# Softmax weights turned by VectorE and transfers within SBUF instead of TensorE transposes

## The chip, the core and the metric

The kernel runs on one core of a Trainium2 chip. A core has TensorE (PE: matrix products into PSUM), VectorE (DVE), ScalarE (ACT), GpSimd (POOL) and SyncE (SP), each with a queue of its own that it works through in order, and 16 DMA engines that move data between memories. PE stands for the matrix products and PEld for the loads of stationary operands that go with them. The metric is the device time of one execution in microseconds (us), lower is better.

## What is computed

One encoder layer over 256 tokens of width 2048, in float32. The part that matters here is the attention group: twelve query heads of 128, four key and value heads (three queries share one), a window of 128 tokens to each side, a bias by distance, and a sink logit in the denominator.

```
q, k, v, u = split(rmsnorm(x) @ w_in)
s = (q @ k.T) * 128**-0.5 - slope * |t - s|        # -1e30 outside the window
m = max(max(s), sink)
p = exp(s - m);  p = p / (sum(p) + exp(sink - m))
out = p @ v                                        # per head: 256 x 256 weights, 256 x 128 values
x = x + concat(rmsnorm(out), rmsnorm(fourier(u))) @ w_out
x = x + conv_ffn(rmsnorm(x));  y = rmsnorm(x)
```

The scores come out with the queries on the partitions, so that the softmax runs along the free dimension. The product with the values sums over the keys, so it needs the weights with the keys on the partitions: each head's 256 x 256 weights have to be transposed once.

## The kernel before

Every float32 product is made of three products of rounded halves: a tensor is split into a high half (a copy to float32r on ScalarE) and a low half (the difference, on VectorE). The weights of the layer come in units of 1 MB: SP loads a unit (`load`, L172, issue in L177) into one of three raw buffers, `split` (L179) has ScalarE write the high half (L185) and VectorE the low one (L186), and TensorE multiplies. The order on every engine is written out by hand. For unit i, `unit(i, work)` (L423) issues what is listed `before` unit i, then unit i's matrix products, then what is listed `beside` it, then the split of unit i + 2 (and with it the load of unit i + 5, as soon as its raw buffer is read), then what is listed `behind` it. Each engine works in this order, so whatever stands in `beside` on VectorE or ScalarE is ahead of the split of unit i + 2.

Units 0 to 3 hold the Fourier input, 4 to 7 the values, 8 to 23 the keys and queries (one k, then three q, four times; `OPENING` and `QK_ORDER`, L45 to L50), 24 to 39 the output projection. A q or k unit is 32 products of 512 or 256 columns (L395, L397). The attention of a head whose q stands in unit s is spread over the units after it (L748 to L778):

- s + 1: the query is added up and split (`qk_out` L633, `qk_parts` L642; the addition is L637, the halves L234 and L235; for a key L637, L639, L652, L653)
- s + 2: the scores, six products (L663), `scores_out` (L671: bias and maximum, L679 to L684) on VectorE, and behind the split the exponentials on ScalarE (`exps`, L687)
- s + 3: `weigh` (L700): VectorE adds the sink, takes the reciprocal (L702, L703) and scales both halves of the weights (L706)
- s + 4: `turn` (L708): four TensorE transposes of 128 x 128 (L713) into one PSUM bank, listed before the unit's products; `turn_out` (L719): ScalarE copies the bank to the high half (L725), VectorE writes the low one (L726)
- s + 5: `values` (L729): six products (L735) ahead of the unit's own; `values_out` writes the head's output as halves (L492, L234, L235).

So every unit of this stage has work of several heads. Below, the heads of one group of three are called A, B and C in order. In `beside` the order before is: the query's `qk_out`, `turn_out`, `weigh`, the key's `qk_out` and `qk_parts`, `scores_out`, `values_out`. The Fourier group (L516 to L590) runs in units 5 to 13 and uses buffers of the tag `sc` as well. The tag `sc` has four buffers of 128 x 512, the halves of the turned weights two each.

Of the kernel before, what the change touches and what calls it, by code (L numbers as in the profile page):

```python
# [8 lines left out]
F32 = mybir.dt.float32  # L9
F32R = mybir.dt.float32r  # L10
AF = mybir.ActivationFunctionType
ALU = mybir.AluOpType

P = 128
D = 2048
S = 256
# [80 lines left out]
def block_kernel(  # L97
# [18 lines left out]
    nc = tc.nc  # L116
# [6 lines left out]
    dn = ctx.enter_context(tc.tile_pool(name="dn", bufs=4, space=bass.MemoryType.PSUM))  # L123

    def f32(ap):
        return ap.bitcast(F32)
# [13 lines left out]
    def bank(pool, name):  # L140
        return pool.tile([P, 512], F32, tag=pool.name, name=name)
# [63 lines left out]
    for n, size in enumerate(U_LOADS[1:], 1):  # L205
        k = sum(U_LOADS[:n])
# [15 lines left out]
    ident = base.tile([P, P], F32, tag="ident", name="ident")  # L222
    make_identity(nc, ident)

    ps = bank(dn, "ps_warm")
# [21 lines left out]
    for c in range(4):  # L247
        t = base.tile([P, 4, 512], F32R, tag=f"hT{c}", name=f"hT{c}")
# [45 lines left out]
    k = 0  # L294
# [15 lines left out]
    ph = pa.enter_context(tc.tile_pool(name="pa", bufs=1))  # L310
# [103 lines left out]
    before, beside, behind = {}, {}, {}  # L414

    def at(when, i, f, *a):
        when.setdefault(i, []).append((f, a))
# [136 lines left out]

    def fourier_rows_out():
        for g in range(NG):
            t = ph.tile([P, 512], F32, tag="sc", name=f"uf{g}", bufs=4)[:, 0:S]
            if g % 2:
                nc.scalar.activation(t, held.pop(("f", g))[:, 0:S], AF.Copy)
            else:  # L560
                nc.vector.tensor_copy(t, held.pop(("f", g))[:, 0:S])
            us.append(t)
# [39 lines left out]
    at(beside, 8, fourier_weights_out)  # L602
    at(before, 7, fourier_rows)
    at(beside, 7, fourier_rows_out)
    at(beside, 8, lambda: rows_out(v_hi, v_lo, ps_v))
    at(behind, 8, distances)

    def fourier_channels_steps():
        for g in range(NG):
            i = 9 + g  # L610
            at(beside, i, fourier_channels_copy, g)
            at(beside, i + 1, fourier_channels_join, g)
            at(behind, i + 1, fourier_channels_out, g)
        at(beside, 15, total_scale, "f", FW)
# [15 lines left out]
    qk_sb, st = {}, {}  # L630
    sq_a = ph.tile([P, S], F32, tag="sq", name="sq_a")

    def qk_out(kind, h, ps):  # L633
        tmp = ph.tile([P, S], F32, tag="tmp", name=f"tmp_{kind}{h}", bufs=2)
        nc.scalar.activation(tmp, ps[:, S : 2 * S], AF.Copy)
        add = ph.tile([P, S], F32, tag="add", name=f"add_{kind}{h}", bufs=2)
        nc.vector.tensor_tensor(add, ps[:, 0:S], tmp, ALU.add)  # L637
        if kind == "k":
            nc.vector.tensor_tensor(add, add, r1b, ALU.mult)  # L639
        st["add", kind, h] = add  # L640
# [30 lines left out]
    def scores_out(h):  # L671

        ps = st.pop(("s", h))
        sc = ph.tile([P, 512], F32, tag="sc", name=f"sc{h}", bufs=4)
        mx = ph.tile([P, 2], F32, tag="mx", name=f"mx{h}", bufs=2)
        neg = ph.tile([P, 2], F32, tag="neg", name=f"neg{h}", bufs=2)
        for b in range(2):
            s = slice(b * S, (b + 1) * S)
            nc.vector.tensor_tensor_reduce(  # L679
                sc[:, s], ps[:, s], rel[:, s], -float(SL[h]), -3e38, ALU.add,  # L680
                ALU.max, mx[:, b : b + 1],
            )
        nc.vector.tensor_tensor(neg, mx, rq_neg, ALU.mult)
        nc.vector.tensor_scalar(neg, neg, sink_neg[:, h : h + 1], None, ALU.min)  # L684
        st["sc", h] = sc, neg
# [20 lines left out]
            nc.vector.tensor_scalar(sc[:, s], sc[:, s], ex[:, b : b + 1], None, ALU.mult)  # L706

    def turn(h):  # L708
        ps = st["t", h] = bank(dn, f"ps_t{h}")
        sc = st.pop(("sc", h))[0]  # L710
        for sb in range(2):
            for b in range(2):
                nc.tensor.transpose(  # L713
                    ps[:, b * S + sb * P : b * S + (sb + 1) * P],
                    sc[:, b * S + sb * P : b * S + (sb + 1) * P],
                    ident,
                )

    def turn_out(h):  # L719
        ps = st.pop(("t", h))  # L720
        pt = [
            ph.tile([P, 512], F32R, tag=f"pt{q}", name=f"pt{q}{h}", bufs=2)
            for q in range(2)
        ]
        nc.scalar.activation(pt[0], ps, AF.Copy)  # L725
        nc.vector.tensor_tensor(pt[1], ps, f32(pt[0]), ALU.subtract)  # L726
        st["p", h] = pt

    def values(h, pool):  # L729
# [19 lines left out]
    for i in range(N_QK, N_OUT + 8):  # L749
        heads = {i - s: h for (kind, h), s in slot_of.items() if kind == "q"}  # L750
        new = [kh for kh, s in slot_of.items() if i - s == 1]
        if i - 9 in range(NG):
            at(before, i, fourier_channels, i - 9)
        if 5 in heads:
            at(before, i, values, heads[5], mm if i < N_OUT else dn)
        if 4 in heads:
            at(before, i, turn, heads[4])
        if i == 15:
            at(before, i, total, sq_f, "f")
        if 2 in heads:  # L760
            at(before, i, scores, heads[2])

        for kind, h in new:
            if kind == "q":
                at(beside, i, lambda k=kind, h=h: qk_out(k, h, st.pop(("ps", k, h))))
        if 4 in heads:
            at(beside, i, turn_out, heads[4])
        if 3 in heads:
            at(beside, i, weigh, heads[3])
        for kind, h in new:  # L770
            if kind == "k":
                at(beside, i, lambda k=kind, h=h: qk_out(k, h, st.pop(("ps", k, h))))
            at(beside, i, qk_parts, kind, h)
        if 2 in heads:
            at(beside, i, scores_out, heads[2])
            at(behind, i, exps, heads[2])
        if 5 in heads:
            at(beside, i, values_out, heads[5])  # L778

    fourier_channels_steps()  # L780
    for n, (kind, h) in enumerate(QK_ORDER):
# [57 lines left out]
    for n, (c, kq) in enumerate(OUT_ORDER):  # L839
        i = N_OUT + n  # L840
# [14 lines left out]
        if kq >= 2:  # L855
            part = "a" if kq == 2 else "f"
            ps = ps_a[c] if kq < 3 else ps_a[c, "f"]
# [307 lines left out]
    for q in range(2):  # L1165
        kind, j = items[q]
        ps = bank(mm, f"ps_{kind}{j}")
# [16 lines left out]
    for n, it in enumerate(items):  # L1184
# [8 lines left out]
        if it[0] in ("gate", "val"):  # L1193
            kind, j = it
            ps = bank(mm, f"ps_{kind}{j}")
# [4 lines left out]
        if it[0] == "product":  # L1200
            kind, g, c, p = it
            hi, lo = halves.pop(it)
            both = c == 2
            shape = (2, 1024) if both else (4, 512)
            for cc in (0, 1) if both else (c,):
# [5 lines left out]
                ps = bank(mm, f"ps_{p}{g}{cc}")  # L1211
# [6 lines left out]
        else:  # L1218
            kind, g, c = it
            hi, lo = halves.pop(up_index[n])  # L1220
            ps = [bank(mm, f"ps_l{g}{c}{b}") for b in range(2)]
# [10 lines left out]
    i = up_index[n]  # L1232
# [156 lines left out]
```

## Time and profile before

| | |
|---|---|
| time, median of 3 runs | 905.74 us (905.70 to 905.91) |
| the profiled execution's own time | 905.91 us |
| its span | 904.1 us |
| mean granted clock of TensorE | 0.998 |
| instructions | 12736 |
| DMA moved | 214.86 MB, mean 238 GB/s |
| SP's queue (q1) | 184.29 MB in 28592 packets |

The profile is one execution. Its page gives the busy time of every engine, and the chain of waits that ended last: followed back from the last instruction, at each step to what released it. The timeline lists instructions with start and duration; what stands in brackets is how long the engine was idle ahead of it, and what ended that. A name such as pt<-ps_t says what is written and what is read, L and a number the line of the kernel. SPq is SP's queue of DMA issues.

### The profile page before, as it was taken

Reading aid. Unit: us, or ns where it says so; the run is one execution under the profiler, and the core shown is the slowest. Engines: PE = TensorE matmul, PEld = TensorE weight load, DVE = VectorE, ACT = ScalarE, POOL = GpSimd, SP = SyncE. Lnnn points to the kernel's source line nnn. Section 1 sums busy time; section 2 is a strip of 40 time slices with the busy share of each in tenths; the row PEclk is TensorE's granted clock in tenths of the full one; section 3 lists DMA queues with packets and bytes.
Section 4 is the critical chain, followed back from the end, with each engine's and each line's share of the span. In section 5 each row is a group of like instructions: output and inputs, shape, how many; then the busy total and the mean of one; then the engine's idle time right before and its main releaser. Section 6 shows DMA issues by size and latency. Waiting matters only on the chain.

```text
span 904.1 us, 12736 instructions
## 1 busy us (share of the span) xinstructions
PE 895.6 (99%) x5064; PEld 808.5 (89%) x5064; DVE 746.0 (83%) x894; ACT 546.7 (60%) x661; POOL 51.6 (6%) x65
## 2 busy tenths in 40 slices
PE   9999999999999999999999999999999999999996
PEld 7899999888899999999999999999999999999885
DVE  7569888666668877889887998878988789998996
ACT  7757677555455656556565565566655566656544
POOL 0001111000000000000000000000000000000004
PEclk9999999999999999999999999999999999999999
DMA  9964544456568678677898779887888988779652
GB/s 359 343 232 142 187 155 171 145 182 227 192 242 272 231 242 252 187 256 235 271 265 271 245 258 285 261 278 238 274 250 244 312 263 263 242 240 289 213 198 94
DMA packets 32908, 214.86 MB, mean 238 GB/s; under 512 B 3632, under 2 KB 4016, under 8 KB 8528
## 3 DMA queue, kind: packets, MB, share of 16 engines
q1 hardware_dynamic: 28592, 184.29, 54.9%
q0 software_dynamic: 4112, 29.49, 17.5%
q8 instruction: 40, 0.66, 0.3%
q10 hardware_dynamic: 144, 0.26, 0.1%
q14 instruction: 20, 0.16, 0.0%
HBM read 211.93 MB, written 2.10 MB: 237 GB/s over the span
## 4 chain that ended last, share of the span: by engine, by line
PE 95%; DVE 2%; POOL 1%; issue 1%; ACT 0%; POOLq 0%; ACTq 0%; DVEq 0%
PE ps_val L395 17%; PE ps_gate L395 17%; PE ps_gate L397 8%; PE ps_val L397 8%; PE ps_q L395 5%; PE ps_P L1106 3%; PE ps_P L1108 3%; PE ps_P L1107 3%; PE ps_N L1106 2%; PE ps_N L1108 2%; PE ps_N L1107 2%; PE ps_u L289 2%; PE ps_q L397 2%; PE ps_a L378 2%; PE ps_a L380 2%; PE ps_a L379 2%
## 5 line engine op out<-in xcount | busy, mean ns | idle before, releaser
L186 DVE TENSOR_TENSOR parts<-raw,parts 128x2048 fp32r<-128x2048 f32 (+1 forms) x129 | 293.2, 2273 | 47.1 <-ACT parts L185 46.4
L185 ACT ACTIVATE parts<-raw 128x2048 fp32r<-128x2048 f32 (+1 forms) x129 | 245.6, 1903 | 44.5 <-PE ps_a L380 12.4
L395 PE MATMUL ps_val<-hU,parts 128*128 128x512 f32 x688 | 227.7, 382 | 0.0
L395 PE MATMUL ps_gate<-hU,parts 128*128 128x512 f32 x688 | 227.3, 382 | 0.0
L397 PE MATMUL ps_val<-hU,parts 128*128 128x256 f32 x688 | 187.5, 273 | 0.0
L397 PE MATMUL ps_gate<-hU,parts 128*128 128x256 f32 x688 | 186.9, 273 | 0.0
L395 PEld LDWEIGHTS ps_val<-hU,parts 128*128 128x128 f32 x688 | 130.0, 189 | 18.1
L395 PEld LDWEIGHTS ps_gate<-hU,parts 128*128 128x128 f32 x688 | 130.0, 189 | 18.1
L397 PEld LDWEIGHTS ps_val<-hU,parts 128*128 128x128 f32 x688 | 132.0, 192 | 0.8
L397 PEld LDWEIGHTS ps_gate<-hU,parts 128*128 128x128 f32 x688 | 131.8, 192 | 0.9
L884 ACT ACTIVATE ft_g<-ps_gate 128x256 f32<-128x256 f32 x43 | 16.5, 384 | 112.5 <-PE ps_gate L397 109.9
L395 PE MATMUL ps_q<-hT,parts 128*128 128x512 f32 x192 | 62.6, 384 | 0.0
L884 ACT ACTIVATE ft_v<-ps_val 128x256 f32<-128x256 f32 x43 | 16.5, 384 | 73.4 <-PE ps_val L397 73.4
L1106 PE MATMUL ps_P<-parts_P,op_P 128*128 128x512 f32 x144 | 54.7, 380 | 0.0
L1107 PE MATMUL ps_P<-parts_P,op_P 128*128 128x512 f32 x144 | 54.6, 379 | 0.0
L1108 PE MATMUL ps_P<-parts_P,op_P 128*128 128x512 f32 x144 | 54.6, 379 | 0.0
L397 PE MATMUL ps_q<-hT,parts 128*128 128x256 f32 x192 | 50.4, 273 | 0.0
L992 DVE TENSOR_TENSOR parts_N<-sumw,parts_N 128x2048 fp32r<-128x2048 f32 x18 | 41.2, 2288 | 9.9 <-ACT parts_N L991 9.9
L1106 PE MATMUL ps_N<-parts_N,op_N 128*128 128x512 f32 x108 | 41.0, 380 | 0.0
L1107 PE MATMUL ps_N<-parts_N,op_N 128*128 128x512 f32 x108 | 40.9, 379 | 0.0
L1108 PE MATMUL ps_N<-parts_N,op_N 128*128 128x512 f32 x108 | 40.9, 379 | 0.0
L395 PEld LDWEIGHTS ps_q<-hT,parts 128*128 128x128 f32 x192 | 36.1, 189 | 4.7
(344 smaller groups left out, 1555.0 us busy)
## 6 DMA issues: line engine op xcount, KB each, us to landing
raw<-in_w_up SPq DMA_DIRECT2D x86, 1024.0 KB, 6.2
raw<-in_w_in SPq DMA_DIRECT2D x20, 1024.0 KB, 4.9
sumw<-in_w_down POOLq DMA_DIRECT2D x18, 1024.0 KB, 8.4
raw<-in_w_out SPq DMA_DIRECT2D x16, 1024.0 KB, 4.8
raw<-in_w_down_late SPq DMA_DIRECT2D x4, 1024.0 KB, 5.3
u_raw<-in_u_in SPq DMA_DIRECT2D x4, 768.0 KB, 10.9
raw<-in_w_down_last SPq DMA_DIRECT2D x4, 768.0 KB, 4.2
u_raw<-in_u_in SPq DMA_DIRECT2D x7, 384.0 KB, 6.4
```

Of the source, the lines that this page charges most:

```text
L185: nc.scalar.activation(hi, raw, AF.Copy)
L186: nc.vector.tensor_tensor(lo, raw, f32(hi), ALU.subtract)
L289: nc.tensor.matmul(ps_u[b], block(hk(k), part, b, True), in_turn(w), start=k == 0 and n == 0, stop=k == NK - 1 and n == 2,)
L378: nc.tensor.matmul(ps, ah, wh, start=first and q == q0, stop=False)
L379: nc.tensor.matmul(ps, al, wh, start=False, stop=False)
L395: nc.tensor.matmul(ps, hi[:, s], in_turn(h), start=k == 0, stop=False)
L397: nc.tensor.matmul(ps[:, 0:S], lo[:, s], in_turn(h)[:, 0:P], start=False, stop=k == NK - 1)
L884: nc.scalar.activation(tmp, ps[:, S : 2 * S], AF.Copy)
L992: nc.vector.tensor_tensor(lo, src, f32(hi), ALU.subtract)
L1106: nc.tensor.matmul(ps, o[:, 0, p, :], wh, start=first and p == 0, stop=False)
L1107: nc.tensor.matmul(ps, o[:, 1, p, :], wh, start=False, stop=False)
L1108: nc.tensor.matmul(ps, o[:, 0, p, :], wl, start=False, stop=end)
```

## The change

`turn` no longer uses TensorE. VectorE transposes the 128 x 512 weights of a head in one instruction, in square blocks of 32: each 32 x 32 block is turned and stays within its band of 32 partitions, and the output pattern puts the blocks of one target band side by side. What is left is to bring each block to its band of partitions: 16 DMAs on SP's queue, each of 32 partitions by 128 elements (16 KB, rows of 512 bytes), from the tile `tb` to the tile `td`. `turn_out` then reads `td` in pieces of 32 elements instead of a PSUM bank.

`weigh` and `turn` now stand together, first in `beside` of unit s + 3. `turn_out` stays in unit s + 4, but is now the last in `beside`, behind `values_out`; `values` stays in s + 5. To make room, `sc` has one buffer instead of four and the low half of the turned weights one instead of two; `tb` and `td` have two each, and the Fourier rows use them before the attention does.

```diff
     def fourier_rows_out():
         for g in range(NG):
-            t = ph.tile([P, 512], F32, tag="sc", name=f"uf{g}", bufs=4)[:, 0:S]
+
+            tag, bufs = [("sc", 1), ("tb", 2), ("tb", 2), ("td", 2)][g]
+            t = ph.tile([P, 512], F32, tag=tag, name=f"uf{g}", bufs=bufs)[:, 0:S]
...
-        sc = ph.tile([P, 512], F32, tag="sc", name=f"sc{h}", bufs=4)
+        sc = ph.tile([P, 512], F32, tag="sc", name=f"sc{h}", bufs=1)
...
     def turn(h):
-        ps = st["t", h] = bank(dn, f"ps_t{h}")
+
+
         sc = st.pop(("sc", h))[0]
-        for sb in range(2):
-            for b in range(2):
-                nc.tensor.transpose(
-                    ps[:, b * S + sb * P : b * S + (sb + 1) * P],
-                    sc[:, b * S + sb * P : b * S + (sb + 1) * P],
-                    ident,
+        t = ph.tile([P, 512], F32, tag="tb", name=f"tb{h}", bufs=2)
+        nc.vector.transpose(
+            t.rearrange("p (k n e) -> p n k e", k=4, e=32),
+            sc.rearrange("p (n k e) -> p n k e", k=4, e=32),
+        )
+        d = st["t", h] = ph.tile([P, 512], F32, tag="td", name=f"td{h}", bufs=2)
+        for a in range(4):
+            for k in range(4):
+                nc.sync.dma_start(
+                    d[32 * k : 32 * (k + 1), P * a : P * (a + 1)],
+                    t[32 * a : 32 * (a + 1), P * k : P * (k + 1)],
                 )
 
     def turn_out(h):
-        ps = st.pop(("t", h))
+
+        d = st.pop(("t", h)).rearrange("p (a n e) -> p n a e", a=4, e=32)
         pt = [
-            ph.tile([P, 512], F32R, tag=f"pt{q}", name=f"pt{q}{h}", bufs=2)
+            ph.tile([P, 512], F32R, tag=f"pt{q}", name=f"pt{q}{h}", bufs=2 - q)
             for q in range(2)
         ]
-        nc.scalar.activation(pt[0], ps, AF.Copy)
-        nc.vector.tensor_tensor(pt[1], ps, f32(pt[0]), ALU.subtract)
+        hi, lo = (t.rearrange("p (n a e) -> p n a e", a=4, e=32) for t in pt)
+        nc.scalar.activation(hi, d, AF.Copy)
+        nc.vector.tensor_tensor(lo, d, f32(hi), ALU.subtract)
         st["p", h] = pt
...
-        if 4 in heads:
-            at(before, i, turn, heads[4])
         if i == 15:
             at(before, i, total, sq_f, "f")
         if 2 in heads:
             at(before, i, scores, heads[2])
+        if 3 in heads:
+            at(beside, i, weigh, heads[3])
+            at(beside, i, turn, heads[3])
...
-        if 4 in heads:
-            at(beside, i, turn_out, heads[4])
-        if 3 in heads:
-            at(beside, i, weigh, heads[3])
...
         if 5 in heads:
             at(beside, i, values_out, heads[5])
+        if 4 in heads:
+            at(beside, i, turn_out, heads[4])
```

## Prediction

> **What bounds the kernel now.** I read the page's busy times first, then its chain of waits, then a table of stretches of the attention stage, then the chain itself and the engines' timelines there.
>
> ```profile
> PE 895.6 (99%) x5064; PEld 808.5 (89%) x5064; DVE 746.0 (83%) x894; ACT 546.7 (60%) x661; POOL 51.6 (6%) x65
> PE 95%; DVE 2%; POOL 1%; issue 1%; ACT 0%; POOLq 0%; ACTq 0%; DVEq 0%
> 101.40:127.70 26.30, 26.30 (x178) 24.61 (x178) 23.28 (x51) 18.82 (x37) 2.41 (x3) 1.00 0.47 161
> 86.90:178.70 91.80, 91.80 (x586) 84.96 (x586) 76.57 (x162) 63.35 (x122) 10.03 (x12) 1.00 0.47 161
> ```
>
> TensorE sets the end nearly everywhere. The columns of the last two rows are length, then busy time of PE, PEld, DVE, ACT and POOL, granted clock, DMA share and GB/s. 101.40 to 127.70 is one period of four units (one k, three q), 6.57 us per unit. VectorE is busy 23.28 of 26.30 us there: 3.0 us are free, 0.76 per unit. So this is a TensorE-bound stage with VectorE close behind, and the change moves work from the one to the other.
>
> **What the turn costs on TensorE.** The chain shows a turn as one piece:
>
> ```profile
> 86.90 0.67 PE ps_o L735 x6
> 101.38 0.67 PE ps_s L663 x6
> 107.29 0.44 PE ps_t L713 x4
> 178.68 0.67 PE ps_o L735 x6
> L713 PE MATMUL ps_t<-ident,sc x48: 272/273/273, 80.4 to 173.2; 128*128 128x128 f32 x48
> ```
>
> The four transposes take 0.44 us of the chain (their records of 273 ns each overlap). Twelve heads: 12 x 0.44 = 5.3 us, all on the path. That is the whole possible gain: 905.91 - 5.3 = 900.6. A two-unit stretch then needs 2 x 6.56 - 1.5 x 0.44 = 12.5 us of TensorE instead of 13.1 (91.80 us over 14 units, of which three in four turn a head).
>
> **What is added to VectorE, and what the new order does.** One 128x512 transpose per head; no row has one.
>
> ```profile
> 102.82 0.62 DVE L706 TENSOR_SCALAR sc<-sc,ex 128x256 f32<-128x256 f32 x2
> 108.39 0.69 DVE L726 TENSOR_TENSOR pt<-ps_t,pt 128x512 fp32r<-128x512 f32 x1 [0.51 <-ACT pt L725]
> 111.72 0.83 DVE L653 TENSOR_TENSOR kT<-add_k,kT 128x256 fp32r<-128x256 f32 x1 [0.93 <-ACT kT L652]
> 103.35 0.46 DVE L235 SCALAR_TENSOR_TENSOR qT<-add_q,qT 128x256 fp32r<-128x256 f32 x1
> ```
>
> The lower bound is two plain passes of 256 elements (L706, 0.62 us for both), the upper one the key's split with its scattered pattern (L653), twice for 512 elements: 1.7. The nearest row has the same size, L726 with 0.69; I take 0.68, so 12 x 0.68 = 8.2 us. The Trainium skill, "VectorE: DVE Perf Modes", section "The three transpose paths", gives 311 ns for a 128x128 transpose of two-byte elements; four such would be 1.24 us, an estimate that would add 12 x 0.56 = 6.7 us of VectorE time to my sum, and no row of this profile shows it.
>
> The two passes of turn_out now read SBUF. The same shapes from SBUF stand in L523 and L524:
>
> ```profile
> L523 ACT ACTIVATE pos_hi<-pos x1: 627/627/627, 38.6 to 38.6; 128x512 fp32r<-128x512 f32 x1
> L524 DVE TENSOR_TENSOR pos_lo<-pos,pos_hi x1: 684/684/684, 39.5 to 39.5; 128x512 fp32r<-128x512 f32 x1
> 107.76 0.60 ACT L725 ACTIVATE pt<-ps_t 128x512 fp32r<-128x512 f32 x1 [0.87 <-PE ps_t L713]
> ```
>
> So nothing changes there (0.03 us on ScalarE), if the pieces of 32 elements cost nothing. The key's scattered split takes 0.83 against a query's 0.46, so 0.7 us per head is the upper bound. Fewer buffers cost nothing: the one left of sc is written by VectorE right behind the transpose that read it, and the one left of the low half is free when the product at the unit's start is done.
>
> The order matters more. Weigh and turn now stand first in a unit's VectorE work, and turn_out last, directly ahead of the split of the next weights. Before, weigh lay between a query's addition and its split, and filled the wait for ScalarE's half. Without it the trace shows a gap:
>
> ```profile
> 70.49 0.48 DVE L235 SCALAR_TENSOR_TENSOR qT<-add_q,qT 128x256 fp32r<-128x256 f32 x1 [0.60 <-ACT qT L234]
> 119.25 2.29 DVE L186 TENSOR_TENSOR parts<-raw,parts 128x2048 fp32r<-128x2048 f32 x1 [0.20 <-ACT parts L185]
> 124.92 2.29 DVE L186 TENSOR_TENSOR parts<-raw,parts 128x2048 fp32r<-128x2048 f32 x1 [0.42 <-ACT parts L185]
> ```
>
> That is 0.60 us for each of three queries in a period, beside the 0.93 of the key that is there already. The split's own wait for ScalarE (0.2 to 0.4 us a unit today) stays, some 1.4 us per period. VectorE's period becomes 23.28 + 3 x 0.68 + 3 x 0.60 + 0.93 + 1.4 = 29.5 us, against 25.0 that TensorE would then need and 26.30 now. VectorE becomes a bound by itself, 14.7 us per two units.
>
> **The transfers.** Each head issues 16 of 16 KB on SP's queue, 192 in all, and all wait for one transpose. Behind them in SP's order stands the load of weights three units ahead.
>
> ```profile
> L199 SPq DMA_DIRECT2D u_raw<-in_u_in x12: 328/432/601, 0.7 to 8.1; - x12
> 0.74 5.07 SPq L199 DMA_DIRECT2D u_raw<-in_u_in  x10
> out_y<-xs SPq DMA_DIRECT2D x8, 256.0 KB, 2.3
> raw<-in_w_in SPq DMA_DIRECT2D x20, 1024.0 KB, 4.9
> L325 SPq DMA_DIRECT2D pos<-in_c_pos x1: 430/430/430, 23.5 to 23.5; - x1
> DMA to landing us min/median/max: 11.4/11.4/11.4
> SPq L199 <- DMA u_raw<-in_u_in: 1.8, 2, 1.4
> SPq L213 <- DMA u_raw<-in_u_in: 4.1, 4, 1.5
> ```
>
> An issue takes 0.33 us at least, and ten back to back took 5.07, 0.51 apart. I take 0.40, because these transfers are small and the lower end is that of single issues. An unhindered landing takes 2.3 us (the stores at the end). So from transpose to last landing: 0.1 + 16 x 0.40 + 2.1 = 8.6 us. Lower bound: 16 x 0.33 + 1.8 = 7.1. Upper bound: 16 x 0.51 + 2.3 = 10.5. The last four rows speak for the upper half. A small load behind megabyte loads took 11.4 us to land, so these go through one line in order, and a weight load issued just ahead (4.9 us) is in the way. The queue also waited for earlier loads to land before it issued more, into buffers that were new: only so many can be under way. The SP queue is occupied for 3 x 16 x 0.40 + 4 x 0.33 = 20.5 of 25 us, so it can just keep up; a late weight load has three units of lead and costs nothing. POOL's queue is not touched.
>
> The Trainium skill, "DMA: Bandwidth & Descriptors", section "Rules for kernel authors", says to merge many small transfers, since under 64 KB one pays mostly overhead. That speaks against pieces of 16 KB, and by it the sum would be the long line's among the rivals.
>
> **The sum.** The waiting instruction is turn_out's copy on ScalarE; behind it on ScalarE stands the split of the next weights, behind that on VectorE their other half, and behind that the weigh and transpose of a later head. So there is a loop over two units: head A's landing holds the turn of head C, two units on, C's that of the next group's A, and so on. Each value product also needs its copy at the start of the unit after.
>
> ```profile
> 103.63 1.93 ACT L185 ACTIVATE parts<-raw 128x2048 fp32r<-128x2048 f32 x1
> 105.59 2.29 DVE L186 TENSOR_TENSOR parts<-raw,parts 128x2048 fp32r<-128x2048 f32 x1 [0.26 <-ACT parts L185]
> 102.43 0.15 DVE L702 TENSOR_TENSOR sm<-sm,ex 128x2 f32<-128x2 f32 x1
> ```
>
> One link: copy 0.50 (start to next start), ScalarE's split 1.96 (103.63 to 105.59), VectorE's 2.21, weigh 0.92 (102.43 to 103.35), transpose 0.68, landing 8.6: 14.9 us for two units, where VectorE alone gives 14.7, TensorE 12.5 and today's stage 13.1. There are seven links, from the first value product at 86.90 to the last at 178.68.
>
> Ahead of them comes an offset. The first product needs the first turn_out, which now follows unit 13's scores:
>
> ```profile
> 82.01 0.68 DVE L726 TENSOR_TENSOR pt<-ps_t,pt 128x512 fp32r<-128x512 f32 x1
> 87.06 0.23 DVE L684 TENSOR_SCALAR neg<-neg,sink_neg 128x2 f32<-128x2 f32 x1
> ```
>
> VectorE ended those scores at 87.2. From that goes the copy that moves (0.6), to that come two transposes (1.24) and a gap (0.6): 88.4. Then the copy, 0.7: 89.1 instead of 86.9, an offset of 2.2 us. After unit 28 the kernel is as before. The product at 178.7 so comes at 86.9 + 2.2 + 7 x 14.9 = 193.4, 14.7 us later. The profiled execution took 905.91 (span 904.1 and 1.8 around it), the median of the three is 905.74: **920.6 us**.
>
> **The rivals.**
> - **The transfers are hidden, VectorE alone is the bound.** For it: 8.6 us is about what VectorE has to do between a turn and its turn_out. Five links of 14.7 while there are queries, two of 12.5 in the output units, where VectorE has gaps such as these, and the offset: 86.9 + 2.2 + 98.5 = 187.6, 8.9 late: 914.8. With no more than today's 3.0 us of gaps in a period, five links of 14.2 and the same rest: 912.
>
> ```profile
> 167.88 0.69 DVE L726 TENSOR_TENSOR pt<-ps_t,pt 128x512 fp32r<-128x512 f32 x1 [2.02 <-ACT pt L725]
> 176.66 2.29 DVE L186 TENSOR_TENSOR parts<-raw,parts 128x2048 fp32r<-128x2048 f32 x1 [1.31 <-ACT parts L185]
> ```
>
> - **The line is long.** Each turn stands behind a weight load and waits for landings: 10.5 us, links of 16.8: 7 x 16.8 + 2.2 - 91.8 = 28: 934.
> - **Faster.** VectorE runs ahead of TensorE by up to two units of split weights; if its gaps close and a landing takes under 12.5 - 6.3 = 6.2 us, no product waits and the 5.3 us are gained: 900.6. The point that decides is 6.2 us of landing, or 0.39 us per issue with no landing time at all; against it, 16 issues of 0.33 alone are 5.3. The Trainium skill, "DMA: Bandwidth & Descriptors", section "Rules for kernel authors", says a transfer issued early and waited for late hides its fixed cost; that is this rival's mechanism.
> - **It cancels.** Links of 13.1 with little offset would land within 0.2% of before, about what a measurement of this kernel can tell from no change.
>
> **How the numbers follow.** My forecast (links of 14 to 16) 0.55, VectorE alone 0.2, the long line 0.12, faster 0.1, cancels 0.03. Faster by over 0.2%: 0.10; within: 0.03; slower: 0.87. For 8 in 10 I leave out the faster and even cases and the far end of the long line: 908 to 934.
>
> **What would show it.** After the change the busy row of TensorE should keep its matmuls but lose share, idle ahead of ps_o (L735 before) for 1 to 3 us per head; 40 or more us of SP issues; turn_out's ScalarE copy waiting for a DMA by name. If ScalarE's copy waits for nothing and VectorE has no gaps, VectorE alone is the bound. If a transfer lands within 6 us of its transpose and TensorE has no idle time, I am wrong altogether. A landing of 12 us or more points to the long line.

## The result, and the profile after

| | before | after |
|---|---|---|
| time, median | 905.74 us (4 runs, 905.70 to 905.91) | 962.99 us (4 runs, 960.93 to 964.14) |
| the profiled execution | 905.91 | 962.98 |
| its span | 904.1 | 961.2 |
| mean granted clock | 0.998 | 0.972 |

The ratio is 1.0629, with an interval of 1.0611 to 1.0648: the change costs 57 us. The sign was forecast, the size was not: 962.99 lies above the range.

From the page of the changed kernel, the busy row, the chain that ended last by engine, and the row of the new transfers (count, size, median time from issue to landing):

```profile
PE 917.7 (95%) x5016; PEld 821.5 (85%) x5016; DVE 754.6 (79%) x906; ACT 546.0 (57%) x661; POOL 54.1 (6%) x65
PE 76%; DVE 6%; SPq 6%; DMA 5%; ACT 4%; issue 2%; POOL 1%; ACTq 0%; POOLq 0%; DVEq 0%
td<-tb SPq DMA_DIRECT2D x192, 16.0 KB, 1.8
```

TensorE's share of the chain falls from 95% to 76%. SP's queue (SPq) and DMA, which were not in it, hold 11%, over 100 us. In the part of the chain from 70 to 240 us the issues of the new transfers (L722) have 31.6% and their landings 4.2%. Another 21.9% are landings of weight loads: there the chain goes back from an issue that waited a moment to the load that it waited for. A single new transfer lands 1.8 us after its issue, which is quick, so it isn't the landing that fills the chain. The table of stretches, one period of four units each:

```profile
77.13:117.54 40.41, 33.13 (x178) 29.29 (x178) 26.46 (x61) 19.64 (x39) 3.67 (x4) 0.87 0.37 116
117.54:158.08 40.54, 30.83 (x158) 27.13 (x157) 24.15 (x53) 18.29 (x36) 2.22 (x3) 0.83 0.38 124
158.08:198.78 40.70, 32.32 (x163) 28.30 (x162) 24.09 (x53) 18.45 (x36) 2.20 (x3) 0.83 0.38 124
```

A period takes 40.4 to 40.7 us instead of 26.3, and no compute engine is full in it: VectorE is busy 24.1 of 40.5 in the second and third. The DMA engines move 116 to 124 GB/s instead of 161. SP's queue shows who is full. Its timeline, start and length of each run of issues:

```profile
77.13 10.08 SPq L722 DMA_DIRECT2D td<-tb  x16
87.31 0.53 SPq L177 DMA_DIRECT2D raw<-in_w_in  x1
87.95 10.71 SPq L722 DMA_DIRECT2D td<-tb  x16
98.76 0.53 SPq L177 DMA_DIRECT2D raw<-in_w_in  x1
99.38 10.20 SPq L722 DMA_DIRECT2D td<-tb  x16
109.68 6.52 SPq L177 DMA_DIRECT2D raw<-in_w_in  x2
117.54 10.43 SPq L722 DMA_DIRECT2D td<-tb  x16
```

Sixteen issues take 10.1 to 10.7 us here, and those of heads A, B and C follow each other, with only a weight load between them, from 77.13 to 109.58. Each issue holds the queue for 0.59 us, and the next starts 0.63 after it:

```profile
L722 SPq DMA_DIRECT2D td<-tb x192: 507/589/1302, 77.1 to 230.3; - x192
DMA to landing us min/median/max: 1.7/1.8/5.4
```

The weight loads are not what fills the rows. In the whole stage the issues of the new transfers waited for landings of weight loads seven times, 2.7 us in all, against 113 us that the 192 issues themselves hold the queue (total, times, longest):

```profile
SPq L722 <- DMA raw<-in_w_in: 1.7, 4, 0.9
SPq L722 <- DMA raw<-in_w_out: 1.0, 3, 0.4
```

The chain tells what closes the period after C's last issue:

```profile
109.00 1.78 DMA td<-tb
111.09 0.63 ACT pt L735
111.72 1.81 ACT parts L185
113.55 2.29 DVE parts L186
116.15 0.63 DVE sc L708 x2
116.80 0.71 DVE tb L715
```

Landing, ScalarE's copy, its split of the next weights, VectorE's half of it, weigh, transpose: the link of the prediction, and then the next group's row of issues at 117.54. C's `turn_out` stands a unit ahead of the next A's `turn`, so the next row can't begin before C's landing. A's landing holds up C's transpose in the same way, but that one is done by 95.87, before B's issues end at 98.66, so it costs nothing. So a period is three rows of issues with a load between them (32.5 us) and one link with a landing (8.0), 40.4 us. The waits of the stage say the same from the other end: ScalarE's copy waits for the transfers, the products for the copy (total, times, longest).

```profile
ACT pt L735 <- DMA td<-tb: 53.3, 12, 8.1
PE ps_o L745 <- ACT pt L735: 31.8, 11, 4.9
```

The last value product starts at 233.57 instead of 178.68 (+54.9), and the rest of the kernel takes 727.6 us instead of 725.4. At its start a product takes 0.43 us for some 4 us, then 0.22:

```profile
233.57 1.44 PE ps_o L745 x5
235.01 0.43 PE ps_ff L378
237.90 0.22 PE ps_ff L379
```

### The profile page after: what moved, and what is told of

The parts are those of the page before. It is cut to its first block, busy times and chain, and to the rows that moved or that the text cites. A ratio compares the mean times of both kernels' runs of the same rounds, so it can differ in the third digit from the quotient of the medians.

```text
span 961.2 us, 12943 instructions
## 1 busy us (share of the span) xinstructions
PE 917.7 (95%) x5016; PEld 821.5 (85%) x5016; DVE 754.6 (79%) x906; ACT 546.0 (57%) x661; POOL 54.1 (6%) x65
## 4 chain that ended last, share of the span: by engine, by line
PE 76%; DVE 6%; SPq 6%; DMA 5%; ACT 4%; issue 2%; POOL 1%; ACTq 0%; POOLq 0%; DVEq 0%
PE ps_val L395 16%; PE ps_gate L395 16%; PE ps_gate L397 8%; PE ps_val L397 8%; SPq L722 6%; PE ps_P L1115 3%; PE ps_P L1117 3%; PE ps_P L1116 3%; DVE parts L186 2%; PE ps_N L1115 2%; PE ps_N L1117 2%; PE ps_N L1116 2%; DMA raw<-in_w_in 2%; PE ps_u L289 2%; ACT parts L185 2%
## 5 line engine op out<-in xcount | busy, mean ns | idle before, releaser
L395 PE MATMUL ps_q<-hT,parts 128*128 128x512 f32 x192 | 71.4, 426 | 0.0
L397 PE MATMUL ps_q<-hT,parts 128*128 128x256 f32 x192 | 53.6, 290 | 0.0
L745 PE MATMUL ps_o<-pt,v_hi 128*128 128x256 f32 x48 | 17.7, 421 | 35.0 <-ACT pt L735 31.8
L395 PEld LDWEIGHTS ps_q<-hT,parts 128*128 128x128 f32 x192 | 41.1, 216 | 6.6
L745 PEld LDWEIGHTS ps_o<-pt,v_hi 128*128 128x128 f32 x48 | 11.0, 255 | 41.4 <-ACT pt L735 35.4
L1115 PE MATMUL ps_N<-parts_N,op_N 128*128 128x512 f32 x108 | 41.0, 380 | 0.0
```

The source lines that it names most:

```text
L395: nc.tensor.matmul(ps, hi[:, s], in_turn(h), start=k == 0, stop=False)
L397: nc.tensor.matmul(ps[:, 0:S], lo[:, s], in_turn(h)[:, 0:P], start=False, stop=k == NK - 1)
L745: nc.tensor.matmul(ps[:, 0:S], v[:, sb, g * HD : (g + 1) * HD], from_halves(pt[q], sb), start=sb == 0 and n == 0, stop=sb == 1 and n == 2,)
L1115: nc.tensor.matmul(ps, o[:, 0, p, :], wh, start=first and p == 0, stop=False)
```

## The experiments

The theory after the result: **the row of issues on SP's queue** is what costs, 0.63 us for each issue, 48 in a row per group of three heads. The rivals: VectorE's transposes and the new order; the bytes of the transfers or their place in line behind the weight loads. "Without turning between bands" below means that the blocks stay in their bands of 32 partitions, which leaves out that part of the computation.

### One transfer per head

```diff
-        for a in range(4):
-            for k in range(4):
-                nc.sync.dma_start(
-                    d[32 * k : 32 * (k + 1), P * a : P * (a + 1)],
-                    t[32 * a : 32 * (a + 1), P * k : P * (k + 1)],
-                )
+        nc.sync.dma_start(d, t)
```

> One transfer of 128 x 512 from tb to td per head takes the place of the 16: the same bytes, one issue; the blocks stay in their own bands, so the turning between bands is left out. Issue theory (each issue holds SP's queue for 0.63 us, 48 of them in a row per group of three heads make the 40.5 us period): 0.6 + 1.8 us from transpose to landing, no wait for a transfer, VectorE is next in line: 908 to 916 us. Rival, VectorE and the new order make the loss: 950 to 963. Rival, bytes of the transfers disturb the weight loads: 950 to 963.

914.25 us, ratio to before 1.0095 (1.0078 to 1.0112). With the same bytes and one issue, 49 of the 57 us are gone. The transfer now lands 4.1 us after its issue, but that is covered. Its issue row, the only wait for a transfer (total, times, longest), and a period:

```profile
L720 SPq DMA_DIRECT2D td<-tb x12: 470/471/525, 77.0 to 179.7; - x12
ACT pt L730 <- DMA td<-tb: 0.7, 1, 0.7
107.92:136.96 29.04, 26.25 (x166) 23.67 (x166) 23.93 (x53) 18.00 (x36) 2.24 (x3) 1.00 0.49 172
```

The period is 29.04 us: this is the bound that VectorE and the order set. The prediction's sum for it was 29.5. That the two are so close is partly luck: VectorE is busy 23.93 us, where the sum has 25.3, and idle for 5.1, where the sum has 4.1.

### No transfer

```diff
-        d = st["t", h] = ph.tile([P, 512], F32, tag="td", name=f"td{h}", bufs=2)
-        for a in range(4):
-            for k in range(4):
-                nc.sync.dma_start(
...
+        st["t", h] = t
```

> No transfers: turn_out reads tb itself; bringing the blocks to their bands is left out, transpose and order stay. Issue theory: as with one transfer or up to 3 us less, 906 to 915 us: what is left over the kernel before is VectorE's own part. Rival, VectorE and order make the loss: 950 to 963. If it falls below 903, VectorE's part is nothing and my VectorE sum (29.5 us per period) was wrong.

915.17 us, ratio 1.0102 (1.0087 to 1.0117), 0.2 us above its expected band. The transfer of the version above is covered in full. The version without it is even 0.9 us slower, which is within the intervals of the two ratios; in the profiled executions the granted clock is 0.991 against 0.997, and whether that is the reason stays open.

### The order alone

The kernel before, with weigh first in `beside` and `turn_out` last; the TensorE transposes stay.

```diff
-        if 4 in heads:
-            at(beside, i, turn_out, heads[4])
-        if 3 in heads:
-            at(beside, i, weigh, heads[3])
+        if 3 in heads:
+            at(beside, i, weigh, heads[3])
...
             at(beside, i, values_out, heads[5])
+        if 4 in heads:
+            at(beside, i, turn_out, heads[4])
```

> The kernel before with only the order changed: weigh first and turn_out last beside a unit, the TensorE transposes stay in front of the unit. My VectorE sum: gaps of 0.6 us per query come in, 8.2 us of transposes do not: 906 to 911 us. Issue theory says nothing on the order: 905 to 911. Rival, the late turn_out makes the loss: over 930.

909.77 us, ratio 1.0043 (1.0028 to 1.0058). The order alone costs 4 us, with no new work anywhere.

### Half of the issues on GpSimd's queue

```diff
-                nc.sync.dma_start(
+                (nc.sync, nc.gpsimd)[k % 2].dma_start(
```

> The same 16 transfers per head, half of them issued by GpSimd's queue, half by SP's. Issue theory: 8 x 0.63 = 5 us per head on SP, landing some 7 us after the transpose, so the period falls from 40.5 to about 29 us and the time to 912 to 925. Rival, the transfers themselves are slow (small rows, or they stand behind the weight loads): 945 to 963.

927.55 us, ratio 1.0239 (1.0224 to 1.0254): the same 192 transfers, 35 us faster than the change. It is not that they land sooner: the median is 2.8 us from SP's queue and 2.6 from GpSimd's, against 1.8 in the change. SP's rows are halved, GpSimd's stand beside them (the POOL row also has the engine's own idle time ahead of it):

```profile
77.39 5.04 SPq L722 DMA_DIRECT2D td<-tb  x8
77.65 3.95 POOL L722 DMA_DIRECT2D td<-tb  x8 [2.27 <-DVE tb L715]
```

It came out 2.5 us above the expected band. The Trainium skill, "DMA: Bandwidth & Descriptors", section "Issuing engines are not separate DMA queues", says that issuing from several engines saves only the sequencer's time to initiate a transfer, usually small beside the transfer. This run fits the first half. The second doesn't hold for this kernel: an issue takes 0.59 us where a transfer lands in 1.8, 48 of them stand in a row, and sharing them out saved 35 us.

### Four transfers, and 32

First four transfers of 128 x 128 per head, without turning between bands; then 32 of 32 x 64.

```diff
+        for k in range(4):
+            nc.sync.dma_start(d[:, P * k : P * (k + 1)], t[:, P * k : P * (k + 1)])
```

> Four transfers of 128 x 128 per head (64 KB each) in place of 16: the same bytes, rows of 512 bytes as before; the turning between bands is left out. If an issue costs the same for any shape (0.47 us for the one of 128 x 512, 0.59 for 32 x 128), SP is held for some 2.5 us per head, the landing comes 4 to 5 us after the transpose and VectorE hides it: 913 to 916 us, as with one transfer. Rival, the cost goes with the number of rows (4 x 128 here, 16 x 32 before: the same 512): 2.5 us per issue, near 963.

915.11 us, ratio 1.0102 (1.0085 to 1.0118).

```diff
-                nc.sync.dma_start(
-                    d[32 * k : 32 * (k + 1), P * a : P * (a + 1)],
-                    t[32 * a : 32 * (a + 1), P * k : P * (k + 1)],
-                )
+                for o in (0, 64):
+                    nc.sync.dma_start(
+                        d[32 * k : 32 * (k + 1), P * a + o : P * a + o + 64],
+                        t[32 * a : 32 * (a + 1), P * k + o : P * k + o + 64],
+                    )
```

> 32 transfers of 32 x 64 per head in place of 16 of 32 x 128: the same bytes, twice the issues, the same result. Issue theory: each added issue costs 0.63 us in full, 12 x 16 x 0.63 = 121 us more, 1084 us (1070 to 1095). Rival, bytes or landings count: 963 to 985.

1084.38 us (one run): 121.4 us more for 192 more issues, 0.632 us each. Issue rows of the four, then of the 32, and one head's run of the 32:

```profile
L721 SPq DMA_DIRECT2D td<-tb x48: 465/596/638, 77.3 to 182.2; - x48
```

```profile
L723 SPq DMA_DIRECT2D td<-tb x384: 507/589/1527, 77.2 to 352.3; - x192
77.16 20.23 SPq L723 DMA_DIRECT2D td<-tb  x32
```

64 KB, 16 KB and 8 KB all take 0.59 to 0.60 us to issue in the median, 128 rows as long as 32. So neither bytes nor rows count here, only the number of issues. The 32 leave the place of the blocks and the bytes as they were, and each issue added costs its full length: SP's queue is the bound of the stage.

### Through HBM: five issues

```diff
+        row = dram.tile([P, 512], F32, tag="turn", name=f"turn{h}", bufs=2)
+        nc.sync.dma_start(row, t)
+        blocks = row.rearrange("(a p) (k f) -> k p a f", a=4, k=4)
+        for k in range(4):
+            nc.sync.dma_start(d[32 * k : 32 * (k + 1)].rearrange("p (a f) -> p a f", a=4), blocks[k])
```

> The blocks go through HBM: one store of the tile, then four loads of 32 partitions each, five issues per head on SP's queue, with the reference's result. Issue theory: 0.5 + 2.3 to the store's landing, 4 x 0.6 of loads, 2 us to the last landing, some 7 us, which fits into the 8 us that VectorE has to do meanwhile: 914 to 922 us. Rival, landings behind the weight loads (5 us each time, for store and loads): 930 to 945.

921.97 us, ratio 1.0181 (1.0166 to 1.0197), at the upper end. One head on SP's queue, then the wait that is left:

```profile
108.29 0.33 SPq L721 DMA_DIRECT2D turn<-tb  x1
112.36 2.69 SPq L724 DMA_DIRECT2D td<-turn  x4
ACT pt L734 <- DMA td<-turn: 14.0, 6, 5.2
```

The queue waits some 4 us for the store to land; then four loads take 2.7 us and land 2.0 later, some 9 us in all. The weight loads are in the way of the store: the loads are issued 2.9 us after the store where a weight load went out 2.5 us before it (77.42), and 5.6 after it where one went out 0.5 us before it (115.62).

### The best case: no transfer, and the order of before

`qk_out`, `turn_out`, `weigh`, `turn`, as the kernel before had it, two buffers for each half, without turning between bands.

```diff
+        if 4 in heads:
+            at(beside, i, turn_out, heads[4])
+        if 3 in heads:
+            at(beside, i, weigh, heads[3])
+            at(beside, i, turn, heads[3])
         for kind, h in new:
             if kind == "k":
...
-        if 4 in heads:
-            at(beside, i, turn_out, heads[4])
```

> VectorE's transposes without any transfer, in the order of before (query addition, turn_out, weigh, turn), with two buffers for both halves; bringing the blocks to their bands is left out. It is the best that the change could give if the transfers cost nothing. If the order makes the rest of the loss: 900 to 904 us, the 5.3 us of TensorE are gained. If VectorE's 0.71 us per head make it (busy 25.4 of a period in which TensorE needs 25.0): 906 to 913.

903.87 us, ratio 0.9981 (0.9971 to 0.9990). This is what the idea is worth if the transfers are free: 2 of the 5.3 us. It lies in the band given for all 5.3, at its upper end. The period of the query units is 26.30 us as before, though TensorE turns nothing in it. From 70 to 146 us the chain now runs through VectorE and ScalarE, and TensorE is in it only from 146.46 on; the 2 us come in the output units, where the last value products stand 5.85 us apart instead of 6.29. And 11 us of the no-transfer version's 915.17 belong to the new order beside the transposes. (That version also has only one buffer for the low half, but its trace has no wait for that buffer.)

```profile
101.00:127.30 26.30, 25.67 (x170) 23.82 (x169) 24.39 (x53) 18.91 (x39) 2.35 (x4) 1.00 0.48 167
```

```profile
170.63 0.67 PE ps_o L739 x6
176.48 0.67 PE ps_o L739 x6
```

### One unit more for the landing

Three versions with the order of before, `turn_out` in unit s + 5 and `values` in s + 6, and two units of the output projection exchanged so that the last heads are there in time.

```diff
-        if 5 in heads:
-            at(before, i, values, heads[5], mm if i < N_OUT else dn)
+        if 6 in heads:
+            at(before, i, values, heads[6], mm if i < N_OUT else dn)
...
-        if 4 in heads:
-            at(beside, i, turn_out, heads[4])
+        if 5 in heads:
+            at(beside, i, turn_out, heads[5])
```

> A version meant to keep the gain: five issues per head through HBM, the order of before (query addition, turn_out, weigh, turn), and turn_out and the value product one unit later each, so that a landing has two units, 13 us, in place of one; two out-projection units change places so that the last heads are there in time. Same result as the reference. Issue theory and VectorE's part as measured without transfers (903.87): a landing of 9 us is covered, 904 to 908 us, at the level of the kernel before or just under it. Rival, the landings take longer than 13 us behind weight loads, or the later product delays the projection: 912 to 925.

Through HBM: 909.77 us, ratio 1.0042 (1.0029 to 1.0056), between the two expected bands.

> The 16 transfers of the change, with turn_out and the value product one unit later and the order of before. It parts SP's throughput from the wait for a landing. If SP's row of issues is the bound by itself, 12 heads x 10.7 us from 77 to 206, then landing, copies and product: the last product some 25 us later than its place: 928 to 938 us. If what costs is one landing's latency inside a unit, the added unit hides it: 905 to 915. If each landing holds up the next head whatever the place of turn_out: 955 to 963.

The 16 transfers: 949.55 us, ratio 1.0481 (1.0467 to 1.0495). This expectation missed all its bands. Its queue (the row at 153.13, the start of the third group, stands apart because six rows between are left out), and what ScalarE and VectorE did in the first gap:

```profile
100.45 10.39 SPq L722 DMA_DIRECT2D td<-tb  x16
110.94 1.00 SPq L177 DMA_DIRECT2D raw<-in_w_in  x2
115.59 10.69 SPq L722 DMA_DIRECT2D td<-tb  x16
```

```profile
153.13 10.02 SPq L722 DMA_DIRECT2D td<-tb  x16
```

```profile
112.37 0.64 ACT pt L735
113.03 0.69 DVE pt L736
114.85 0.71 DVE tb L715
```

The queue isn't in use from 111.94 to 115.59. In this order C's `turn_out`, which waits for C's landing, stands ahead of the next A's transpose, so the row of issues still pauses for a landing once per group: 37.5 us per period (115.59 to 153.13) instead of 40.5. The added unit, with the order of before, took 3 us from each period and left the three rows of issues. The expectation for the row of issues alone had counted no pause between the groups.

> The same order with turn_out and product one unit later and no transfers at all; bringing the blocks to their bands is left out. It says what the later place costs by itself: 903.5 to 905 if nothing (903.87 without the delay), 908 to 911 if it is what the version through HBM lost.

Without a transfer: 905.22 us, ratio 0.9995 (0.9986 to 1.0004), 0.2 above the band for no cost. The later place, with the exchanged units and one buffer of the low half, costs 1.4 us by itself, little more than the noise. So of the 5.9 us that the version through HBM lies above the best case, some 4.5 are the way through HBM.

> The version through HBM with turn_out and product one unit later, its store and four loads now issued by GpSimd's queue, which holds no weight loads in this stage. If the 4 us that the same version on SP's queue lost are the store's wait in the line of the weight loads (landings of 4 to 6.6 us there): 903.9 to 906. If they come from the later product and the changed order of the projection units: 909 to 911, as on SP's queue. Rival, GpSimd's queue issues and lands more slowly, and its sums of squares come late: over 912.

Through HBM on GpSimd's queue: 916.66 us, ratio 1.0105 (1.0090 to 1.0120), the rival's case. The store no longer stands behind weight loads in a line and lands in 3.1 us instead of 4.2, but the loads land later, 4.3 us instead of 2.0, and the waits of the copies grow (SP's version first, then GpSimd's). Whether late sums of squares on GpSimd add to it was not separated.

```profile
td<-turn SPq DMA_DIRECT2D x48, 64.0 KB, 2.0
ACT pt L734 <- DMA td<-turn: 14.6, 4, 4.9
```

```profile
td<-turn POOLq DMA_DIRECT2D x48, 64.0 KB, 4.3
ACT pt L734 <- DMA td<-turn: 21.9, 7, 8.8
```

None of the versions that bring the blocks to their bands beats the kernel before.

## Why the prediction was wrong

- **TensorE's 5.3 us:** the transposes leave the chain as said; without transfers and with the old order 2 us of it are seen. The rest is lost because VectorE is then the bound of the query units, as that version's chain shows. Right in direction.
- **VectorE's part:** right in its prices. The transpose takes 0.711 us (0.68 taken), the copies from SBUF 0.63 and 0.69 as priced, the gap ahead of a query's split 0.50 to 0.63 (0.60 taken). The period without the row of issues was 29.04 (29.5, with the two errors named above that nearly cancel), and the rival "VectorE alone" stood at 914.8, where one transfer gives 914.25. The estimate of 1.24 us from the 311 ns of the Trainium skill, "VectorE: DVE Perf Modes", section "The three transpose paths", would have been too much: 0.71 us decides.

```profile
L715 DVE STREAM_TRANSPOSE tb<-sc x12: 711/711/712, 76.4 to 216.4; 128x512 f32<-128x512 f32 x12
78.00 0.48 DVE L235 SCALAR_TENSOR_TENSOR qT<-add_q,qT 128x256 fp32r<-128x256 f32 x1 [0.58 <-ACT qT L234]
89.25 0.69 DVE L736 TENSOR_TENSOR pt<-td,pt 128x512 fp32r<-128x512 f32 x1 [1.05 <-ACT pt L735]
```

- **The offset:** within a microsecond, in part by luck. The first low half starts at 89.25, forecast for 88.4 (where the sum has 1.24 for two transposes, twice 0.68 is 1.36). VectorE was ready for it at 88.20, as forecast, but then waited 1.05 us for ScalarE's copy, which had waited for the transfers.
- **The transfers: this step failed.** "I take 0.40, because these transfers are small", with 0.51 as upper bound. An issue holds the queue for 0.59 us and the next starts after 0.63, and its size has nothing to do with it. From that the second fault follows: "so it can just keep up", 20.5 of 25 us. With 0.63 the three rows and the loads need 32.5, more than TensorE's 25, so B's and C's issues wait for A's, and the loop is over a group and not over two units.
- **The link** held in form: from the end of C's last issue to the next group's first it is 8.0 us, against 0.1 + 2.1 + 6.3 = 8.5. But it comes once per period, behind three rows, where the prediction had two links per period. The prediction's formula with 0.63 in it would give 12.3 for a landing, 18.6 for a link and 946 us. The result lies 42 us above the forecast of 920.6: the price of an issue makes 25 of them, and the other 17 come from the queue that three heads share.
- **The long line**, 934, priced a landing behind the weight loads. Those waits are there (the longest landing is 5.4 us), but they add only 2.7 us to all the rows together. The sign named for this rival, 12 us or more from transpose to landing, did appear for B and C (for B from 84.91 to 100.10, when ScalarE's copy could start), and for another reason: B's issues waited for A's. The sign doesn't tell a queue that is full of issues from one that waits for landings; the waits of the queue do.
- **Faster** failed on the point named for it: it needed at most 0.39 us per issue.

## What to carry to other kernels

Count the issues of a queue per period before anything else: number times spacing, over all heads that share the queue, against the period of the engine that bounds the stage. If the profile has no row for a cost, here an issue within SBUF, the true price can lie beyond the nearest row: 0.63 us, where the upper bound was 0.51. With 192 of them, that one price decides the result, so it is worth a run of its own. In an order written out by hand, the place of small instructions (here `weigh` ahead of a query's addition and `turn_out` ahead of a weight split) can cost as much as the work that was moved: 4 us alone, 11 beside the transposes.

## What the runs showed of the hardware

An issue from SBUF to SBUF held SP's queue for 0.59 to 0.60 us in the median when it stood in a row of others (128 x 128, 32 x 128 and 32 x 64 alike), and for 0.47 us when it stood alone (128 x 512) or was the first of four (128 x 128, at 108.36). One from SBUF to HBM or back took 0.34 and 0.43 in the median. GpSimd's queue took 0.50 for the same 32 x 128. TensorE's granted clock fell to 0.83 in a stage in which it waited for a fifth to a quarter of the time, and its products took 0.43 us instead of 0.22 for some 4 us after it.

```profile
L724 SPq DMA_DIRECT2D td<-turn x48: 307/426/1102, 80.3 to 191.0; - x48
L721 SPq DMA_DIRECT2D turn<-tb x12: 326/338/617, 77.4 to 184.1; - x12
```

```profile
L722 POOL DMA_DIRECT2D td<-tb x96: 496/497/547, 77.7 to 189.1; - x96
```
